# Two transformer blocks on one core: operand casts queued behind the next block's taps, half of a key projection between the scores, first loads on two queues

## The chip, the cores and the metric

One Trainium2 chip (trn2), one of its cores. The metric is the device time of one execution in microseconds, the median of several. Weights and activations are float32.

## What is computed

The reference runs two blocks on one sequence of 256 rows and 1024 columns. The first has two layers of a SwiGLU feed-forward, a mixer of three attentions (stick-breaking, forgetting, memory) with gates and an output projection, and a second SwiGLU feed-forward. The second has a mixer by short causal convolutions, a feed-forward with a three-tap causal convolution (d_ff 2816) before its activation, latent attention (keys and values projected up from a narrow latent, rotary parts apart), and that feed-forward once more.

```python
def _swiglu(t, w_gate, w_up, w_down):
    return (jax.nn.silu(t @ w_gate) * (t @ w_up)) @ w_down
...
        log_beta = jax.nn.log_sigmoid(z)
        log_not = jnp.where(mask, log_beta - z, 0.0)
        log_between = lax.cumsum(log_not, axis=3, reverse=True) - log_not
        w = jnp.where(mask, jnp.exp(log_beta + log_between), 0.0)
```

## The kernel before

All matrix products are taken in float32 accuracy from operands split in two parts, hi + lo, each of type fp32r: product = hi·hi + lo·hi + hi·lo, three matmuls where one would do. A weight travels in chunks of 128x1024: SP issues its DMA into a ring of 5 raw buffers, ACT casts it (`hi`, L270), DVE subtracts (`lo`, L271), into rings of 8. 256 rows make two row blocks t=0, 1. A row-wise product (`mm_a`, L302 to L305, into `acc` banks) takes an operand block as the stationary side and 512 weight columns; a column-wise one (`mm_b`, L313 to L315, into `mm`, `gu` or `cf` banks) gives transposed results of 128 columns by 256 rows. Activations are split likewise: `split` casts on ACT (L392, `acth`) and subtracts (L393, `actl`) on DVE or GpSimd (POOL). Four `mm` banks, two `z` banks for scores and two `tr` banks for transposes make up the eight PSUM banks.

The order on PE is written by a planner, `Program`: steps are generators (`spawn`), which yield a delay in nanoseconds of planned PE time (`DELAY`, L169 to L173), while `tick` advances that time with each matmul issued and `join` makes the main program wait for a step. A larger delay therefore puts more matmuls of the main program in front of a step. The other engines' orders are set by a scheduler, which keeps to a few written rules (`issue_after`).

The places that the change touches:

- The table `DELAY` and `HEAD0` (L169 to L176): `sb_z`, `sb_ln`, `sb_cum`, `sb_last` are the delays of the stick-breaking attention; `lat_p` is one in the latent attention.
- `conv_ffn` (L955 on): 22 blocks c of 2 x 128 columns. `finish` lets ACT do the first tap (`conv3_last`, L893) and DVE the other two (`conv3_rest`, L898), both read from the PSUM bank `cf`, then ACT the activation (L974). `gated` multiplies on GpSimd (L978) and, after a further delay, casts the result for the down-projection (`split`: ACT L392, GpSimd L393). The first four blocks come by another way (a row-wise product and transposes), the other 18 column-wise. The function runs twice, l = 0 and l = 1. After it `out_proj` begins row-wise accumulations in banks that become free.
- `conv_mixer` ends with `out_proj` (L953); `tail` and `head` say how many chunks at the end and the start are done for one row block ahead of the other.
- `latent` (L1078 on): `cols_b(s_uk, ...)` projects eight blocks of keys `kn`, `rows(cq, uqr, 1, 512)` is the rotary query part of t=1. `latent_scores` (L1147, L1150) makes the scores of four units (e, t), head group e and row block t; the softmax is on DVE and ACT (L576), then probabilities are transposed on PE (`tr<-ident,p`, L400), copied by ACT (`pT`, L589), and multiplied with the values (`tr<-pT,mv`, L595).
- `run` (L1196 to L1234) is the start: load the input rows, `ident` (for transposes) and `g`, transpose, and split. `across` (L491) waits for the row scales of a norm.

Of the kernel before, what the change touches and what calls it, by code (L numbers as in the profile page):

```python
# [2 lines left out]

# [1 line left out]

# [4 lines left out]
F32 = mybir.dt.float32  # L10
F32R = mybir.dt.float32r
AF = mybir.ActivationFunctionType
ALU = mybir.AluOpType
# [4 lines left out]
P = 128  # L18
# [3 lines left out]
KD = D // P  # L22
# [107 lines left out]
class Act:  # L130
# [14 lines left out]
    def part(self, k, n, t):  # L145

        ts = slice(t * P, t * P + P)
        return [x[k // 4][:, k % 4:k % 4 + n, ts] for x in (self.hi, self.lo)]
# [10 lines left out]
class Program:  # L159
# [7 lines left out]
    NG = 3  # L167
    FINE = 2
    DELAY = dict(fox_norm=3300, att_norm=3300, lat_norm=3300, f=3000, merge=3000, scale=4500, across=9000, first=4000,  # L169
                 fox_pT=3600, att_pT=3600, lat_pT=3600, sb_z=13000, sb_ln=6000, sb_cum=6000, sb_next=1000, sb_last=13000, sb_w=8000,  # L170
                 decay=8000, fox_gap=7000, fox_p=13900, mem_gap=3000, mem_p=19500, mem_norm=17000, conv0=2200, conv_gap=3000,
                 cf_gap=4100, cf_gated=2000, cf_split=9500, kv=5500, q=4000, rope=5600, lat_gap=6000, lat_p=9000, n_conv=9000,
                 n_ffnA=5500, n_mla=7500, n_ffn10=14900, n_ffn11=8100, n_mix=8300, n_ffn20=8300, n_ffn21=6500)  # L173
    TAIL = 8
    HEAD = 8
    HEAD0 = 1  # L176
    OHEAD = 2
    WARM = 2

# [305 lines left out]
    def across(self, r, ready):  # L485

        rb = self.sp.tile([P, S], F32, tag="rb", bufs=1, name="rb")

        def make():
            nc = self.nc  # L490
            yield from self.wait(*ready, *self.scales)  # L491
            self.scales = []
            ds = []
            for t in range(NT):
                d = self.sp.tile([P, P], F32, tag="diag", bufs=2, name="diag")
                nc.vector.tensor_scalar(out=d, in0=self.ident, scalar1=r[:, t:t + 1], scalar2=None, op0=ALU.mult)
                ds.append(d)
            yield self.DELAY["across"]
            ps = self.tr_bank()
            for t in range(NT):  # L500
                nc.tensor.matmul(ps[:, t * P:t * P + P], self.ones32, ds[t], start=True, stop=True)
            nc.vector.tensor_copy(out=rb, in_=ps[:, :S])

        return rb, self.spawn(make())
# [385 lines left out]
    def conv3_last(self, y, ps, col):  # L890


        self.nc.scalar.mul(out=y, in_=ps, mul=self.pp[:, col + 2:col + 3])  # L893

    def conv3_rest(self, y, ps, col):

# [8 lines left out]
    def conv_mixer(self, x, r, ready, nxt):  # L905
        nc = self.nc
        cols = lambda I, a, b: [I["a_w_in_2"][0][:, D * i + a:D * i + b] for i in (1, 2, 0)]
        head = self.weights("a_in0", KD, 768, lambda I: _side_by_side(cols(I, 0, 256)))
        src = self.weights("a_in", 18, 1024, lambda I: _woven(cols(I, 256, D)))
        dsrc = self.weights("a_out", KD, D, lambda I: _by_k(I["a_w_out_2"][0]))  # L910
        y = Act(self, KD)
        ps = [[self.mm_bank("ca"), self.mm_bank("cb")[:, :S]] for _ in range(NT)]
        outs = [[(p[0], slice(0, 512)), (p[1], slice(512, 768))] for p in ps]
        rows = []

        def first(t):
            cc, p, b = [self.t2(name=n)[:, :S] for n in ("cc", "cp", "cb")]
            nc.scalar.mul(out=cc, in_=ps[t][0][:, :S], mul=r[:, t:t + 1])
            nc.vector.scalar_tensor_tensor(out=p, in0=ps[t][0][:, S:], scalar=r[:, t:t + 1], in1=cc, op0=ALU.mult, op1=ALU.mult)
            nc.scalar.mul(out=b, in_=ps[t][1], mul=r[:, t:t + 1])  # L920
            rows.append((p, b))
            if t:
                self.spawn(second(), self.DELAY["conv0"])

        def finish(c, p, b):
            z = self.t2(name="cz")[:, :S]
            self.conv3(z, p, PP_ACONV + 3 * c)
            nc.vector.tensor_tensor(out=z, in0=b, in1=z, op=ALU.mult)
            return z

        def second():
            for c in range(2):
                s = slice(c * P, c * P + P)
                ps = self.transposed(*[rows[t][i][:, s] for i in range(2) for t in range(NT)]).rearrange("p (i t) q -> p i (t q)", i=2)
                self.split([d[:, 0] for d in y.blocks(c, 1)], finish(c, ps[:, 0], ps[:, 1]), nc.gpsimd)
                yield self.DELAY["conv_gap"]

        rb, made = self.across(r, ready)
        self.rows_a(self.whole(head, KD), outs, x, first, head=self.HEAD, ready=ready)
        self.join(made)  # L940
        for c in range(2, KD):
            bank, bank2 = self.mm_bank("cv"), self.mm_bank("cv")
            parts = [bank[:, :S], bank[:, S:], bank2[:, :S]]
            for i in range(3):
                self.mm_b(parts[i], x, *self.take(src, 3 * (c - 2) + i), KD)
            cc, p = [self.t2(name=n)[:, :S] for n in ("cc", "cp")]
            nc.vector.tensor_tensor(out=cc, in0=parts[0], in1=rb, op=ALU.mult)
            nc.vector.tensor_tensor(out=p, in0=parts[1], in1=cc, op=ALU.mult)
            nc.gpsimd.tensor_tensor(out=p, in0=p, in1=rb, op=ALU.mult)
            z = finish(c, p, parts[2])  # L950
            nc.gpsimd.tensor_tensor(out=z, in0=z, in1=rb, op=ALU.mult)
            self.split([d[:, 0] for d in y.blocks(c, 1)], z, nc.gpsimd)
        return self.out_proj(dsrc, KD, y, None, nxt)  # L953

    def conv_ffn(self, l, x, ready, nxt):  # L955


        nc = self.nc
        cols = lambda I, a, b: [I["ffn_w_up_2"][l][:, DFF * i + a:DFF * i + b] for i in range(2)]
        head = self.weights(f"cf_up0{l}", KD, 1024, lambda I: _side_by_side(cols(I, 0, 512)))  # L960
# [3 lines left out]
        ps, outs = self.banks(2)  # L964
        rows = []

        made = {}

        def finish(c, gu):
            y = self.t2(name="cy", shape=(2, S))  # L970
            for part in (self.conv3_last, self.conv3_rest):
                for i in range(2):
                    part(y[:, i], gu[:, i], PP_FCONV + 132 * l + 3 * (c + KF * i))
            nc.scalar.activation(out=y[:, 0], in_=y[:, 0], func=AF.Silu)  # L974
            made[c] = [self.spawn(gated(c, y), self.DELAY["cf_gated"])]

        def gated(c, y):
            nc.gpsimd.tensor_tensor(out=y[:, 0], in0=y[:, 0], in1=y[:, 1], op=ALU.mult)  # L978
            yield self.DELAY["cf_split"]
            self.split([d[:, 0] for d in hT.blocks(c, 1)], y[:, 0], nc.gpsimd)  # L980

        def first(t):
            gu = [self.t2(name=n) for n in ("cg", "cu")]
# [34 lines left out]
    def latent(self, x, ready, nxt):  # L1018
# [56 lines left out]
        put = lambda dst, eng: (lambda b, ps: eng(out=dst[b // 4][:, b % 4:b % 4 + 2], in_=ps))  # L1075
        self.join(*tkv)
        kn = [self.t4(name="kn") for _ in range(2)]
        self.cols_b(s_uk, range(8), ckv, 2, 4, put(kn, nc.vector.tensor_copy))  # L1078
        self.join(*tq)
        tr.append(self.spawn(qrope(1, rows(cq, uqr, 1, 512))))  # L1080
        qn = [self.t4(name="qn") for _ in range(2)]
# [4 lines left out]
        self.v_done = []  # L1086
        units, second = [[], []], []
        scores = self.spawn(self.latent_scores(units, second, qn, kn, qr, kr, v, x))
        self.cols_b(s_uqn, range(4, 8), cq, 4, 2, put(qn, nc.scalar.copy))
        second.append(True)  # L1090
        ps3, outs3 = self.banks(2)
# [76 lines left out]
    def run(self, out):  # L1168
# [28 lines left out]

        def rows(t):
            for a in range(2):
                cs = slice(a * 512, a * 512 + 512)  # L1200
                nc.sync.dma_start(out=self.h[t][:, cs], in_=xin[t * P:t * P + P, cs])
                if t == a == 0:
                    nc.sync.dma_start(out=self.ident, in_=ident)
                    nc.sync.dma_start(out=g, in_=gd)
            yield 0
            for a in range(2):
                ps = self.transposed(self.h[t][:, a * 512:a * 512 + 512])
                hi, lo = x.part(4 * a, 4, t)
                if t or a:
                    self.split((hi, lo), self.gained(ps, g[:, 4 * a:4 * a + 4]), nc.gpsimd)  # L1210
                    continue
                for i in range(4):
                    gc = g[:, i:i + 1]
                    nc.scalar.mul(out=hi[:, i], in_=ps[:, i], mul=gc)
                    nc.vector.scalar_tensor_tensor(out=lo[:, i], in0=ps[:, i], scalar=gc, in1=hi[:, i].bitcast(F32),
                                                   op0=ALU.mult, op1=ALU.subtract)
            self.scales.append(self.spawn(scale(t), self.DELAY["scale"]))

        def scale(t):
# [4 lines left out]
        def warm(n):  # L1224
            ps = self.z_bank()
            for _ in range(n):
                nc.tensor.matmul(ps[:, :P], self.ones32, self.ones32, start=True, stop=True)

        self.tc.keep_in_program_order(nc.scalar.preload_act_table_set("silu_and_others"))
        ready = [self.spawn(rows(0))]  # L1230
        self.join(*ready)
        warm(self.WARM)
        ready.append(self.spawn(rows(1)))
        self.join(*ready)  # L1234
        state = (x, r, ready)
        for l in range(DEPTH):
            state = self.layer(l, *state, consts if l == 0 else None)
# [102 lines left out]
```

## Time and profile before

| | us |
|---|---|
| median of 3 runs (lowest, highest) | 1896.1 (1895.66, 1896.51) |
| the profiled execution | 1896.99 |
| its span | 1895.2 |
| mean granted TensorE clock, share of full | 0.994 |
| PE, DVE, ACT, POOL busy | 1858.4, 1235.9, 966.7, 228.5 |
| read from HBM | 339.05 MB, 180 GB/s over the span |

Busy times of the four engines are those of the profiled execution. PE's busy time holds all of its matmuls, at whichever clock they ran; the difference to the span, 37 us, is time in which PE stood still. A matmul's duration overlaps that of the next, so work is measured from start to start.

### The profile page before, as it was taken

Reading aid. Unit: us, or ns where it says so; the run is one execution under the profiler, and the core shown is the slowest. Engines: PE = TensorE matmul, PEld = TensorE weight load, DVE = VectorE, ACT = ScalarE, POOL = GpSimd, SP = SyncE. Lnnn points to the kernel's source line nnn. Section 1 sums busy time; section 2 is a strip of 40 time slices with the busy share of each in tenths; the row PEclk is TensorE's granted clock in tenths of the full one; section 3 lists DMA queues with packets and bytes.
Section 4 is the critical chain, followed back from the end, with each engine's and each line's share of the span. In section 5 each row is a group of like instructions: output and inputs, shape, how many; then the busy total and the mean of one; then the engine's idle time right before and its main releaser. Section 6 shows DMA issues by size and latency. Waiting matters only on the chain.

```text
span 1895.2 us, 30338 instructions
## 1 busy us (share of the span) xinstructions
PE 1858.4 (98%) x11982; PEld 1665.5 (88%) x11982; DVE 1235.9 (65%) x1657; ACT 966.7 (51%) x1496; POOL 228.5 (12%) x205
## 2 busy tenths in 40 slices
PE   8999999999999999999999999999999989999988
PEld 7998999778899889989987889988989978779976
DVE  6664756767766476637776776647668656648653
ACT  6444545554644364436555454436456545537552
POOL 1000102001100010001200110001404311003320
PEclk9999999999999999999999999999999999999999
DMA  8655655445555555556533655556555454426551
GB/s 282 220 198 190 222 203 177 143 134 202 210 184 185 178 211 189 181 176 237 186 134 130 214 196 189 185 173 210 183 189 178 167 179 157 148 90 201 172 175 64
DMA packets 95357, 343.13 MB, mean 181 GB/s; under 512 B 10720, under 2 KB 10992, under 8 KB 95216
## 3 DMA queue, kind: packets, MB, share of 16 engines
q1 hardware_dynamic: 95216, 341.20, 52.9%
q8 instruction: 94, 1.54, 0.3%
q14 instruction: 47, 0.39, 0.1%
HBM read 339.05 MB, written 2.11 MB: 180 GB/s over the span
## 4 chain that ended last, share of the span: by engine, by line
PE 39%; DVE 5%; issue 2%; ACT 2%; POOL 2%; DMA 0%; DVEq 0%; POOLq 0%; ACTq 0%
PE acc L302 7%; PE acc L305 7%; PE acc L303 6%; DVE cy L898 2%; POOL cy L978 2%; PE gu L314 2%; PE gu L315 2%; PE gu L313 2%; DVE lo L271 2%; ACT hi L270 2%; PE cf L314 2%; PE cf L315 2%; PE cf L313 2%; PE tr L400 1%; PE cv L314 1%
## 5 line engine op out<-in xcount | busy, mean ns | idle before, releaser
L271 DVE TENSOR_TENSOR lo<-raw,hi 128x1024 fp32r<-128x1024 f32 (+3 forms) x609 | 748.0, 1236 | 360.9 <-ACT hi L270 359.6
L270 ACT CAST hi<-raw 128x1024 fp32r<-128x1024 f32 (+3 forms) x609 | 633.1, 1044 | 439.6 <-PE acc L305 212.4
L302 PE MATMUL acc<-hi,acth 128*128 128x512 f32 x1176 | 473.8, 403 | 13.5 <-DVE cy L898 11.8
L303 PE MATMUL acc<-lo,acth 128*128 128x512 f32 x1176 | 466.3, 396 | 0.2 <-DVE lo L271 0.2
L305 PE MATMUL acc<-hi,actl 128*128 128x512 f32 x1176 | 378.9, 397 | 1.8 <-DVE actl L393 1.8
L315 PE MATMUL gu<-acth,lo 128*128 128x256 f32 x1152 | 324.0, 281 | 0.0
L314 PE MATMUL gu<-actl,hi 128*128 128x256 f32 x1152 | 323.8, 281 | 0.0
L313 PE MATMUL gu<-acth,hi 128*128 128x256 f32 x1152 | 323.5, 281 | 0.0
L302 PEld LDWEIGHTS acc<-hi,acth 128*128 128x128 f32 x1176 | 222.8, 189 | 68.0 <-ACT cy L974 13.5
L305 PEld LDWEIGHTS acc<-hi,actl 128*128 128x128 f32 x1176 | 221.9, 189 | 55.8 <-DVE actl L393 4.1
L303 PEld LDWEIGHTS acc<-lo,acth 128*128 128x128 f32 x1176 | 222.9, 190 | 49.5 <-DVE lo L271 0.9
L313 PEld LDWEIGHTS gu<-acth,hi 128*128 128x128 f32 x1152 | 217.1, 188 | 0.2
L314 PEld LDWEIGHTS gu<-actl,hi 128*128 128x128 f32 x1152 | 217.0, 188 | 0.2
L315 PEld LDWEIGHTS gu<-acth,lo 128*128 128x128 f32 x1152 | 217.0, 188 | 0.0
L417 POOL TENSOR_TENSOR r<-v,mhalf 128x1 f32<-128x1 f32 x40 | 52.9, 1322 | 966.9 <-DVE v L414 955.9
L313 PE MATMUL cf<-acth,hi 128*128 128x256 f32 x576 | 162.3, 282 | 0.0
L315 PE MATMUL cf<-acth,lo 128*128 128x256 f32 x576 | 162.1, 281 | 0.0
L314 PE MATMUL cf<-actl,hi 128*128 128x256 f32 x576 | 161.9, 281 | 0.0
L313 PE MATMUL mm<-acth,hi 128*128 128x256 f32 x432 | 122.7, 284 | 0.0
L314 PE MATMUL mm<-actl,hi 128*128 128x256 f32 x432 | 121.6, 281 | 0.0
L315 PE MATMUL mm<-acth,lo 128*128 128x256 f32 x432 | 121.5, 281 | 0.0
L313 PEld LDWEIGHTS cf<-acth,hi 128*128 128x128 f32 x576 | 108.7, 189 | 0.1
(225 smaller groups left out, 2285.6 us busy)
## 6 DMA issues: line engine op xcount, KB each, us to landing
raw<-ffn_gu SPq DMA_DIRECT2D x175, 512.0 KB, 4.3
raw<-ffn_dn SPq DMA_DIRECT2D x88, 512.0 KB, 3.3
raw<-cf_up SPq DMA_DIRECT2D x88, 512.0 KB, 3.5
raw<-gate SPq DMA_DIRECT2D x48, 512.0 KB, 3.3
raw<-cf_dn SPq DMA_DIRECT2D x44, 512.0 KB, 3.5
raw<-a_in SPq DMA_DIRECT2D x18, 512.0 KB, 4.7
gain<-gains SPq DMA_DIRECT2D x17, 512.0 KB, 4.7
raw<-in_v SPq DMA_DIRECT2D x16, 516.0 KB, 4.4
```

The source lines that it names most:

```text
L270: self.last_hi = nc.scalar.copy(out=hi[:, cs], in_=raw[:, cs])
L271: nc.vector.tensor_tensor(out=lo[:, cs], in0=raw[:, cs], in1=hi[:, cs].bitcast(F32), op=ALU.subtract)
L302: nc.tensor.matmul(ps, x.h(k, ts), hi[:, cs], start=first, stop=False)
L303: nc.tensor.matmul(ps, x.h(k, ts), lo[:, cs], start=False, stop=False)
L305: nc.tensor.matmul(ps, x.l(k, ts), hi[:, cs], start=False, stop=last)
L313: nc.tensor.matmul(ps, hi[:, c], x.h(k), start=k == 0, stop=False)
L314: nc.tensor.matmul(ps, hi[:, c], x.l(k), start=False, stop=False)
L315: nc.tensor.matmul(ps, lo[:, c], x.h(k), start=False, stop=k == nk - 1)
L400: self.nc.tensor.transpose(ps[:, w * P:w * P + P], n[:, c * P:c * P + P], self.ident)
L417: nc.gpsimd.tensor_tensor(out=r, in0=v, in1=self.mhalf, op=ALU.pow)
L898: self.nc.vector.scalar_tensor_tensor(out=y[:, i:], in0=ps[:, :S - i], scalar=self.pp[:, col + 2 - i:col + 3 - i], in1=y[:, i:], op0=ALU.m ...
L978: nc.gpsimd.tensor_tensor(out=y[:, 0], in0=y[:, 0], in1=y[:, 1], op=ALU.mult)
```

## The change

Six edits. In `conv_ffn` the cast of block c's product (`split` in `gated`) is issued behind the taps of block c+1 on ACT, if those are known. In `latent`, key blocks 4 to 7 are projected after the scores have been spawned, and `lat_p` is a microsecond of planned time shorter. Four stick-breaking delays are longer. `conv_mixer`'s output projection has tail 6 and head 2. `across` waits first for the operands and then for the scales. At the start, `ident`, `g` and the second row block are loaded by ACT's queue, all four quarters are split by the plain `split` (low halves on DVE), the second row block's transposes are a step with a delay of its own that isn't joined, and `HEAD0` is 3.

```diff
-                 fox_pT=3600, att_pT=3600, lat_pT=3600, sb_z=13000, sb_ln=6000, sb_cum=6000, sb_next=1000, sb_last=13000, sb_w=8000,
+                 fox_pT=3600, att_pT=3600, lat_pT=3600, sb_z=13500, sb_ln=7000, sb_cum=7000, sb_next=1000, sb_last=15000, sb_w=8000,
...
-                 cf_gap=4100, cf_gated=2000, cf_split=9500, kv=5500, q=4000, rope=5600, lat_gap=6000, lat_p=9000, n_conv=9000,
-                 n_ffnA=5500, n_mla=7500, n_ffn10=14900, n_ffn11=8100, n_mix=8300, n_ffn20=8300, n_ffn21=6500)
+                 cf_gap=4100, cf_gated=2000, cf_split=9500, kv=5500, q=4000, rope=5600, lat_gap=6000, lat_p=8000, n_conv=9000,
+                 start=1300, n_ffnA=5500, n_mla=7500, n_ffn10=14900, n_ffn11=8100, n_mix=8300, n_ffn20=8300, n_ffn21=6500)
...
-    HEAD0 = 1
+    HEAD0 = 3
...
-            yield from self.wait(*ready, *self.scales)
+            yield from self.wait(*ready)
+            yield from self.wait(*self.scales)
...
-        self.nc.scalar.mul(out=y, in_=ps, mul=self.pp[:, col + 2:col + 3])
+        self.last_tap = self.nc.scalar.mul(out=y, in_=ps, mul=self.pp[:, col + 2:col + 3])
...
-        return self.out_proj(dsrc, KD, y, None, nxt)
+        return self.out_proj(dsrc, KD, y, None, nxt, tail=6, head=2)
...
-        made = {}
+        made, taps = {}, {}
...
+            taps[c] = self.last_tap
             nc.scalar.activation(out=y[:, 0], in_=y[:, 0], func=AF.Silu)
             made[c] = [self.spawn(gated(c, y), self.DELAY["cf_gated"])]
...
             yield self.DELAY["cf_split"]
-            self.split([d[:, 0] for d in hT.blocks(c, 1)], y[:, 0], nc.gpsimd)
+            with self.tc.issue_after(taps[c + 1].ins) if c + 1 in taps else nullcontext():
+                self.split([d[:, 0] for d in hT.blocks(c, 1)], y[:, 0], nc.gpsimd)
...
-        self.cols_b(s_uk, range(8), ckv, 2, 4, put(kn, nc.vector.tensor_copy))
+        self.cols_b(s_uk, range(4), ckv, 2, 4, put(kn, nc.vector.tensor_copy))
...
         scores = self.spawn(self.latent_scores(units, second, qn, kn, qr, kr, v, x))
+        self.cols_b(s_uk, range(4, 8), ckv, 2, 4, put(kn, nc.vector.tensor_copy))
...
             for a in range(2):
-                cs = slice(a * 512, a * 512 + 512)
-                nc.sync.dma_start(out=self.h[t][:, cs], in_=xin[t * P:t * P + P, cs])
-                if t == a == 0:
-                    nc.sync.dma_start(out=self.ident, in_=ident)
-                    nc.sync.dma_start(out=g, in_=gd)
+                ps = self.transposed(self.h[t][:, a * 512:a * 512 + 512])
+                self.split(x.part(4 * a, 4, t), self.gained(ps, g[:, 4 * a:4 * a + 4]))
             yield 0
-            for a in range(2):
-                ps = self.transposed(self.h[t][:, a * 512:a * 512 + 512])
-                hi, lo = x.part(4 * a, 4, t)
-                if t or a:
-                    self.split((hi, lo), self.gained(ps, g[:, 4 * a:4 * a + 4]), nc.gpsimd)
-                    continue
-                for i in range(4):
-                    gc = g[:, i:i + 1]
-                    nc.scalar.mul(out=hi[:, i], in_=ps[:, i], mul=gc)
-                    nc.vector.scalar_tensor_tensor(out=lo[:, i], in0=ps[:, i], scalar=gc, in1=hi[:, i].bitcast(F32),
-                                                   op0=ALU.mult, op1=ALU.subtract)
...
+        nc.scalar.dma_start(out=self.ident, in_=ident)
+        nc.scalar.dma_start(out=g, in_=gd)
+        for t, a in ((0, 0), (0, 1), (1, 0), (1, 1)):
+            cs = slice(a * 512, a * 512 + 512)
+            (nc.scalar if t else nc.sync).dma_start(out=self.h[t][:, cs], in_=xin[t * P:t * P + P, cs])
...
         warm(self.WARM)
-        ready.append(self.spawn(rows(1)))
-        self.join(*ready)
+        ready.append(self.spawn(rows(1), self.DELAY["start"]))
```

What moves on ACT in the middle of the convolutional feed-forward, between one block's taps (`cy<-cf,pp`) and the next's. Before (line numbers after the change are one to four higher):

```order
L893 ACTIVATE cy<-cf,pp 128x256 x2
L270 CAST hi<-raw 128x1024
L974 ACTIVATE cy<-cy 128x256
L392 CAST acth<-cy 128x256
L270 CAST hi<-raw 128x1024
L893 ACTIVATE cy<-cf,pp 128x256 x2
```

With the change:

```order
L894 ACTIVATE cy<-cf,pp 128x256 x2
L392 CAST acth<-cy 128x256
L270 CAST hi<-raw 128x1024
L976 ACTIVATE cy<-cy 128x256
L270 CAST hi<-raw 128x1024
L894 ACTIVATE cy<-cf,pp 128x256 x2
```

The operand cast has moved from behind its block's activation to behind the next block's taps; the two weight casts are still there, one on either side of the activation.

The second place is ACT at the end of the latent scores: `p` is a softmax activation, `z_16603` and `z_16604` (before) and `z_16599` and `z_16600` (after) are the scores of the last unit, `pT` the copies of transposed probabilities, `acth` the operand of the output projection. Before:

```order
L576 ACTIVATE p_16572,sums_16571<-z_16552,m_16570 128x128 x2
L589 COPY pT_16615<-tr_16616 128x256
L589 COPY pT_16620<-tr_16621 128x256
L589 COPY pT_16625<-tr_16626 128x512
L589 COPY pT_16632<-tr_16633 128x512
L576 ACTIVATE p_16641,sums_16640<-z_16603,m_16639 128x256 x2
L392 CAST acth_16397<-tr_16659 128x2x128
L576 ACTIVATE p_16648,sums_16647<-z_16604,m_16646 128x256 x2
L392 CAST acth_16397<-tr_16664 128x2x128
```

With the change:

```order
L1099 COPY mv_16358<-acc11_16516 128x512
L270 CAST hi_16827<-raw_16826 128x1024
L577 ACTIVATE p_16613,sums_16612<-z_16599,m_16611 128x256 x2
L577 ACTIVATE p_16620,sums_16619<-z_16600,m_16618 128x256 x2
L590 COPY pT_16625<-tr_16626 128x256
L590 COPY pT_16630<-tr_16631 128x256
L590 COPY pT_16635<-tr_16636 128x512
L590 COPY pT_16642<-tr_16643 128x512
L392 CAST acth_16359<-tr_16655 128x2x128
```

The last unit's softmax activations have moved ahead of the four copies; the casts of the first results follow without an activation between them.

The third place is PE at the same scores. `z` are the scores of the second head group, first of t=0 (128x128), then of t=1 (128x256), and `acc` the value projection between them. Before:

```order
L1150 MATMUL z<-kr,qr 128x128 x2
L302 MATMUL acc_16519<-hi,acth 128x512
L303 MATMUL acc_16519<-lo,acth 128x512
L302 MATMUL acc_16520<-hi,acth 128x512
L303 MATMUL acc_16520<-lo,acth 128x512
L305 MATMUL acc_16519<-hi,actl 128x512
L305 MATMUL acc_16520<-hi,actl 128x512
L1147 MATMUL z<-kn,qn 128x256 x2
```

With the change the first six accumulations read the same, and twelve more follow before the scores, of which the last six and the scores are:

```order
L302 MATMUL acc_16515<-hi,acth 128x512
L303 MATMUL acc_16515<-lo,acth 128x512
L302 MATMUL acc_16516<-hi,acth 128x512
L303 MATMUL acc_16516<-lo,acth 128x512
L305 MATMUL acc_16515<-hi,actl 128x512
L305 MATMUL acc_16516<-hi,actl 128x512
L1151 MATMUL z<-kn,qn 128x256 x2
```

Eighteen accumulations now lie between the two pairs of scores, where there were six.

## Rows read from the trace of the kernel before

**Rows 1.** The page, part 1: busy us, share of the span, instructions.

```profile
PE 1858.4 (98%) x11982; PEld 1665.5 (88%) x11982; DVE 1235.9 (65%) x1657; ACT 966.7 (51%) x1496; POOL 228.5 (12%) x205
```

**Rows 2.** PE's waits over the whole run: us in total, times, longest us.

```profile
PE acc L302 <- DVE cy L898: 11.8, 3, 5.5
...
PE tr L641 <- DVE lnl L393: 1.7, 4, 0.6
PE acc L302 <- ACT acth L392: 1.6, 3, 0.7
...
PE z L609 <- DVE lnl L393: 0.9, 2, 0.4
```

**Rows 3.** Timeline of PE, conv_ffn's end: start, us, operation, xcount, [idle before <-releaser].

```profile
1523.11 0.63 PE L305 MATMUL acc<-hi,actl 128*128 128x512 f32 x2
...
1524.17 0.39 PE L303 MATMUL acc<-lo,acth 128*128 128x512 f32 x1
1530.02 0.77 PE L302 MATMUL acc<-hi,acth 128*128 128x512 f32 x1 [5.47 <-DVE cy L898]
```

**Rows 4.** Timeline of ACT, the last block of the same loop.

```profile
1520.54 0.83 ACT L893 ACTIVATE cy<-cf,pp 128x256 f32<-128x256 f32 x2
...
1525.45 0.40 ACT L392 CAST acth<-cy 128x256 fp32r<-128x256 f32 x1 [2.14 <-POOL cy L978]
1525.76 1.04 ACT L270 CAST hi<-raw 128x1024 fp32r<-128x1024 f32 x1
1526.71 0.83 ACT L893 ACTIVATE cy<-cf,pp 128x256 f32<-128x256 f32 x2
1529.07 0.42 ACT L974 ACTIVATE cy<-cy 128x256 f32<-128x256 f32 x1 [1.52 <-DVE cy L898]
```

**Rows 5.** Timeline of DVE, the last block's two other taps.

```profile
1527.98 1.90 DVE L898 SCALAR_TENSOR_TENSOR cy<-cf,pp,cy 128x255 f32<-128x255 f32 x4
```

**Rows 6.** Table of stretches: us, PE, PEld, DVE, ACT, POOL (instructions), PEclk, DMA share, GB/s.

```profile
1500.00:1518.00 18.00, 18.00 (x154) 18.00 (x154) 11.74 (x19) 10.34 (x18) 6.41 (x7) 1.00 0.50 171
...
1530.00:1534.20 4.20, 4.18 (x10) 3.33 (x11) 1.02 (x1) 1.45 (x2) 1.45 (x2) 0.50 0.15 60
...
1650.30:1653.50 3.20, 3.20 (x10) 1.72 (x10) 0.74 (x2) 0.00 (x0) 0.00 (x0) 0.50 0.48 164
...
1831.40:1834.50 3.10, 3.09 (x7) 2.46 (x8) 0.00 (x0) 1.41 (x2) 1.47 (x2) 0.50 0.22 89
1691.00:1694.60 3.60, 3.60 (x10) 2.79 (x11) 3.06 (x4) 0.00 (x0) 1.46 (x1) 0.53 0.86 279
```

**Rows 7.** Timeline of PE, the stick-breaking sums of the first layer.

```profile
342.90 0.51 PE L641 MATMUL tr<-lnh,tri 128*128 128x512 f32 x1 [0.34 <-ACT lnh L392]
343.94 0.51 PE L641 MATMUL tr<-lnl,tri 128*128 128x512 f32 x1 [0.54 <-DVE lnl L393]
```

**Rows 8.** Timeline of PE, the last latent scores.

```profile
1647.45 0.70 PE L1147 MATMUL z<-kn,qn 128*128 128x256 f32 x2 [0.70 <-ACT p L576]
1649.59 0.70 PE L1147 MATMUL z<-kn,qn 128*128 128x256 f32 x2 [1.43 <-ACT p L576]
```

**Rows 9.** Timeline of ACT, first copies of probabilities and the last softmax activations.

```profile
1654.64 0.65 ACT L589 COPY pT<-tr 128x256 f32<-128x256 f32 x2 [5.11 <-PE tr L400]
...
1656.78 0.49 ACT L576 ACTIVATE p<-z,m 128x256 f32<-128x256 f32 x1
```

**Rows 10.** Timelines of PE and DVE, transposes of the query's second row block.

```profile
1613.00 0.60 PE L400 MATMUL tr<-ident,nrm 128*128 128x128 f32 x4
...
1615.44 0.68 DVE L393 TENSOR_TENSOR actl<-tr,acth 128x512 fp32r<-128x512 f32 x1
```

**Rows 11.** Timeline of PE, the start of the second convolutional feed-forward.

```profile
1690.85 0.95 PE L305 MATMUL acc<-hi,actl 128*128 128x512 f32 x2 [0.88 <-DVE actl L393]
```

**Rows 12.** Timelines of SP (DMA issues) and PE at the start.

```profile
2.10 1.38 SPq L1201 DMA_DIRECT2D h<-x  x3
...
11.01 0.78 PE L302 MATMUL acc<-hi,acth 128*128 128x512 f32 x1
```

More of the change, by code (lines that the diff above doesn't have):

```diff
@@ L1 @@
 import math
-from contextlib import ExitStack
+from contextlib import ExitStack, nullcontext
 import numpy as np
```

## The prediction

> **What bounds the kernel now.** I read the engines' busy times first: TensorE (PE) is busy 98% of the span, the next engine 65% [rows 1]. The change takes no matmul away, so it can win only the time in which PE stands still and what it loses at half clock. The list of PE's waits comes second: 11.8 us in three waits at one line, then waits of 1 to 3 us in all at each of several places [rows 2]. Third come the timelines around these waits and the table of stretches. Its column PEclk is the granted clock: 1.00, the 2.4 GHz level, in a stretch without gaps, and 0.50 to 0.53, the 1.2 GHz level, for 4.2, 3.1, 3.2 and 3.6 us behind places where PE had just stood idle [rows 6]. Half of such a stretch is lost, so each wait is priced together with the slow stretch behind it.
>
> The sum is made against the profiled execution, 1896.99 us; the median of the three runs is 0.9 us lower, so I take the saving off 1896.1. A measurement of this kernel can tell about 0.2% (3.8 us) from no change.
>
> **1. The casts in the convolutional feed-forward (15.4 us).** It runs twice. For blocks 4 to 21, 18 in each, PE does 48 matmuls of 128x256, 5.6 us (18 us for 154 of them, 0.117 each [rows 6]). ACT starts to empty a block's bank with its taps (L893), and DVE's two other taps free it [rows 5]. ACT's cycle is longer than PE's: taps start at 1520.54 and at 1526.71, 6.17 us apart, though the work in between is 0.83 + 0.42 + 0.40 and two weight casts of 1.04, 3.7 us. The rest is ACT standing still, 2.14 us of it in the operand cast, which waits for GpSimd's product with a weight cast and the next taps queued behind it [rows 4]. A lag of 0.57 us per block gives 10 us in 18 blocks, and so late the last bank comes free. PE has 24 accumulations to do in the other banks, 5.6 us (two take 0.63 with 0.39 for one, so 0.235 each), ends them at 1524.5 and stands 5.47 us, until 1530.02 [rows 3]; the second pass shows the same wait with one of 0.86 ahead of it, 11.8 in all [rows 2].
>
> The change holds the cast of block c back until the taps of block c+1. The product was there 4.9 us after its block's taps (1525.45 - 1520.54); the next taps come 5.6 us after them, and the cast 6.4 us, so it meets a finished product with 1.5 us to spare, and ACT's cycle falls towards its 3.7 us of work, below PE's 5.6: ACT follows PE. From the start of the last taps to PE's restart the trace has 3.3 us (1526.71 to 1530.02); with a weight cast of 1.04 in front the bank is free 4.3 us after the last block, inside the 5.6 us of accumulations. So 11.8 us of waits go, and half of the slow stretches of 4.2 and 3.1 us: 3.65. **Gain 15.4.** Ends: 8 if half the lag stays, 15.8 with the ragged restart. The cover: the cast, and two weight casts a block behind it, now wait in ACT for PE's next block. By the order of instructions eight weight chunks are cast ahead of each taps, as before, and a block uses two, so PE doesn't feel it. GpSimd's subtraction for the low half moves a block later too; its reader comes tens of us later, and the last block, which has no next taps, isn't held.
>
> **2. Stick-breaking delays (4.5 us).** PE waits 1.7 + 0.9 us for DVE's log terms [rows 2] and 0.34 in each of two layers for ACT's [rows 7], 3.3 in all. A wait costs about half as much again at the restart: from 342.90 to 343.94 are 1.04 us where 0.235 is usual, 0.8 lost for a wait of 0.54. That makes 4.8. By the order the new delays put six or more matmuls, 0.7 to 1.4 us, before each place, more than any one wait. What follows in the mixer comes some 7 us later, and 12 us of accumulations still stand before its last gate, 19 before. **Gain 4.5**, ends 2 and 4.8.
>
> **3. The start (1.3 us).** Each DMA issue costs SP 0.46 us (three in 1.38). `ident`, `g` and the second row block leave its queue, so the second half of the first block is issued 0.9 us sooner and the weights 1.8 us sooner; the first accumulation, now at 11.01 us, no longer has the second block's transposes ahead of it [rows 12]. The bytes are the same. **Gain 1.3**, ends -0.5 (ACT issues four DMAs ahead of its table load) and 3. The Trainium skill, "DMA: Bandwidth & Descriptors", section "Issuing engines are not separate DMA queues", says that transfers started by several engines share the same 16 DMA engines and interleave, and that only the time of issuing is saved. If by that sentence the first loads are limited by transfer, this part is worth 0 and the sum is 1872.8; no row here shows two issuing engines.
>
> **4. From the convolution mixer to its feed-forward (1.0 us).** PE's waits for ACT's operand casts are 1.6 us in three [rows 2], one of them here, 0.7, with two smaller ones behind it. Head 2 and tail 6 leave 36 instead of 48 accumulations behind the first row block and bring the second's transposes 15 rows forward. Ends -1 (less cover for the first norm) and 1.9 (all); I take the middle on the side of a gain, since the casts stand behind weight casts that come sooner now.
>
> **5. From the latent attention to its feed-forward (2.4 us).** Another 0.7 of those casts, then 0.88 us for the low halves [rows 11], then 3.6 us at 0.53, of which 1.7 are lost [rows 6]. Twelve more accumulations (2.8 us) of the second row block now stand behind the first one's end, to cover its norm. All of it would be 3.2; I take 2.4, ends 0 and 3.2.
>
> **6. The latent scores (0).** Saved: PE waits 0.70 and 1.43 us before the last scores [rows 8], as the softmax of the scores before still holds the banks. Half of the key projection moves behind the scores' start, so 18 accumulations (4.2 us) stand there instead of 6 (1.4). The 3.2 us at 0.50 behind it give 1.6 [rows 6]. Together 3.7. Added: ACT runs the last scores' four softmax activations, about 0.6 us each from 1656.78, ahead of the probabilities' copies, which stood at 1654.64 [rows 9]. PE's products need these copies, so they come 3.0 us later; as the activations no longer lie among the later copies and casts, 1.3 come back: +1.7. Transposes and products alternate in other pieces: +0.5. And the key projection's 24 matmuls (2.8 us) are gone from in front of the query's second row block: only 9 follow its transposes, so PE wants the operand at 1613.60 + 9 x 0.117 = 1614.7, and DVE ended it at 1616.12 [rows 10]; with one copy less on DVE I take +1.1 of the 1.4. The clock may fall behind such a wait: half of the 1.6, +0.8. So 4.1 against 3.7: I take **0**; ends a loss of 5 (nothing saved but the waits, all added prices and a slow stretch as before) and a gain of 4.
>
> **Sum:** 15.4 + 4.5 + 1.3 + 1.0 + 2.4 + 0 = 24.6; 1896.1 - 24.6 = **1871.5 us**. The parts lie in different stages, so they add.
>
> **Rivals.**
> *Latent attention gets worse.* The copies behind the activations cost the end of part 6. For: the order puts four activations first; against: PE has 2.8 us more of other work near there. 1871.5 + 5 = 1876.5.
> *The feed-forward's waits only halve.* ACT also waits 1.52 us in its block for DVE's taps [rows 4], and this stays. Against: without the 2.14 its cycle is 6.17 - 2.14 = 4.0, below 5.6. Gain 8 instead of 15.4: 1879, up to 1883 with the clock.
> *Two queues give nothing,* by part 3: 1872.8. For: the same bytes; against: 1.8 us of issuing are gone from SP.
> *All is cured,* upper ends of parts 1 to 5 and half of part 6's: 15.8 + 4.8 + 3 + 1.9 + 3.2 + 2 = 30.7, 1865.5.
> *Slower: weight casts stuck behind a cast that waits for PE.* Place: ACT in the 36 blocks. If fewer than two weight chunks were cast ahead at the taps, PE would stand each block for taps, cast and weight cast, 0.83 + 0.40 + 1.04 = 2.27 us [rows 4], 82 us in all: 1953. That number of two decides. Against: the order has eight, in both programs.
>
> **How the numbers follow.** Forecast 0.50 (1867 to 1875.5); two queues give nothing 0.12; latent worse 0.17; halved 0.11; all cured 0.07; slower 0.03. The range leaves out the slower case, the far half of the halved one and some of the tails: 1863.5 to 1881. Faster by over 0.2% is everything but the slower case and a tail of the halved one in which the small parts turn: 0.95; within 0.2%: 0.02; slower 0.03.
>
> **What would show it.** Right: accumulations wait under 1 us in all on `cy`, ACT's taps stand 5.6 us apart, and no 0.50 stretch follows either pass; PE's waits on the log terms are below 1 us; the first accumulation starts near 9.5 us; the waits before the last latent scores are gone, and one of 2 to 3 us on the copies of the probabilities has come. Wrong: taps still 6 us apart, weight casts that PE waits for in the blocks, or over 5 us lost between the latent scores and the output projection.

## The result and the profile after

| | before | changed |
|---|---|---|
| median (lowest, highest), us | 1895.92 (1895.66, 1896.51) | 1877.58 (1876.01, 1878.95) |
| profiled execution, us | 1896.99 | 1876.01 |

The ratio is 0.9903, 95% interval 0.9885 to 0.9920: 18.3 us faster, 15.2 to 21.8 by the interval. 24.6 us were forecast. The changed kernel's four runs lie 3 us apart and the profiled one is the fastest, so the profile's own saving, 21.0 us, is on the high side. One execution of c_only below took 2258.49 us at a granted clock of 0.753; its figures are those of the other three.

The engines of the changed kernel, page, part 1 [rows 1]:

```profile
PE 1850.2 (99%) x11982; PEld 1664.7 (89%) x11982; DVE 1241.3 (66%) x1658; ACT 965.8 (52%) x1493; POOL 228.5 (12%) x202
```

PE's waits of the changed kernel (us in all, times, longest) [rows 2]:

```profile
PE tr L400 <- DMA ident<-ident: 4.4, 1, 4.4
PE acc L302 <- ACT acth L392: 4.3, 3, 1.7
PE tr L400 <- ACT pT L590: 3.5, 1, 3.5
PE lat L305 <- DVE actl L393: 1.1, 1, 1.1
PE acc L302 <- DVE cz L929: 1.0, 1, 1.0
```

The 11.8 us on `cy` and all waits on the log terms (`lnl`, `lnh`) are gone. New are 3.5 us on the copies of probabilities, 1.1 us in the latent projection, 1.0 us on `cz` in the convolution mixer, and 2.7 us more for ACT's operand casts.

PE where the feed-forward's blocks end in the down-projection; before, 5.47 us of waiting and 4.2 us at half clock lay here [rows 3]:

```profile
1514.73 0.40 PE L302 MATMUL acc<-hi,acth 128*128 128x512 f32 x1
...
1519.84 0.63 PE L305 MATMUL acc<-hi,actl 128*128 128x512 f32 x2
```

ACT near the end of the same loop [rows 4]:

```profile
1502.99 0.83 ACT L894 ACTIVATE cy<-cf,pp 128x256 f32<-128x256 f32 x2
1503.71 0.40 ACT L392 CAST acth<-cy 128x256 fp32r<-128x256 f32 x1
1504.86 1.05 ACT L270 CAST hi<-raw 128x1024 fp32r<-128x1024 f32 x1 [0.75 <-PE cf L314]
1505.82 0.41 ACT L976 ACTIVATE cy<-cy 128x256 f32<-128x256 f32 x1
1507.74 1.05 ACT L270 CAST hi<-raw 128x1024 fp32r<-128x1024 f32 x1 [1.51 <-PE cf L314]
1508.69 0.83 ACT L894 ACTIVATE cy<-cf,pp 128x256 f32<-128x256 f32 x2
```

Taps stand 5.70 us apart instead of 6.17, the cast waits for nothing, and ACT now stands idle until PE's matmuls release a weight buffer (`<-PE cf`): it is ahead of PE, not late.

The table of stretches of the changed kernel (PE, PEld, DVE, ACT, POOL, PEclk, DMA, GB/s) shows the clock behind both passes and at the start of the second feed-forward at 1.00 where rows 6 had 0.50 to 0.53. Behind the new latent wait it is 0.69:

```profile
1518.00:1530.00 12.00, 12.00 (x53) 9.72 (x52) 6.13 (x5) 5.66 (x6) 1.18 (x2) 1.00 0.47 162
1815.00:1825.00 10.00, 10.00 (x44) 8.07 (x44) 6.13 (x5) 4.34 (x5) 0.00 (x0) 1.00 0.77 254
1643.00:1646.00 3.00, 2.64 (x16) 2.11 (x13) 1.02 (x2) 1.52 (x4) 0.00 (x0) 0.69 0.00 0
1678.00:1682.00 4.00, 3.88 (x17) 3.19 (x18) 3.05 (x6) 2.11 (x5) 1.63 (x1) 1.00 0.91 364
```

### The profile page after: what moved, and what is told of

Its sections match the earlier page's. It is cut to its first block, busy times and chain, and to the rows that moved or that the text cites. A ratio compares the mean times of both kernels' runs of the same rounds, so it can differ in the third digit from the quotient of the medians.

```text
span 1873.9 us, 30344 instructions
## 1 busy us (share of the span) xinstructions
PE 1850.2 (99%) x11982; PEld 1664.7 (89%) x11982; DVE 1241.3 (66%) x1658; ACT 965.8 (52%) x1493; POOL 228.5 (12%) x202
## 4 chain that ended last, share of the span: by engine, by line
PE 94%; DVE 3%; issue 2%; ACT 1%; DMA 1%; POOL 0%; DVEq 0%; POOLq 0%; ACTq 0%
PE acc L302 14%; PE acc L305 14%; PE acc L303 14%; PE gu L314 7%; PE gu L315 7%; PE gu L313 7%; PE cf L314 4%; PE cf L315 4%; PE cf L313 4%; PE mm L313 3%; PE mm L315 3%; PE mm L314 3%; PE tr L400 2%; DVE lo L271 1%; PE tr L596 1%
## 5 line engine op out<-in xcount | busy, mean ns | idle before, releaser
L302 PE MATMUL acc<-hi,acth 128*128 128x512 f32 x1176 | 472.5, 402 | 5.3 <-ACT acth L392 4.3
L302 PEld LDWEIGHTS acc<-hi,acth 128*128 128x128 f32 x1176 | 221.3, 188 | 58.8 <-ACT acth L392 6.0
```

The costliest lines, as they stand in the source:

```text
L302: nc.tensor.matmul(ps, x.h(k, ts), hi[:, cs], start=first, stop=False)
```

## The experiments

Twelve kernels in three groups of four, each group on one chip with the kernel before beside it (medians 1896.74, 1896.57, 1896.55). "Saved" is against that median. An edit undone in the changed kernel is compared with the changed kernel's second measurement, `again`.

Differences of 2 to 3 us between these kernels need care, because the start of the program varies by as much from profile to profile. In the first feed-forward 825 matmuls into `gu` follow each other without a matmul of another kind. I divide every profile at the first of them. The first of these lines is from the changed kernel's first profile, the second from again, the third from no_head, and up to there all three run the same instructions:

```profile
40.29 0.37 PE L313 MATMUL gu<-acth,hi 128*128 128x256 f32 x1
...
42.38 0.36 PE L313 MATMUL gu<-acth,hi 128*128 128x256 f32 x1
...
39.94 0.37 PE L313 MATMUL gu<-acth,hi 128*128 128x256 f32 x1
```

Profiles by this division (the runs are explained below):

| profile | first of these matmuls at, us | from there to the start of the last matmul, us |
|---|---|---|
| before | 41.5 | 1846.5 |
| changed, first profile | 40.3 | 1826.4 |
| changed, again | 42.4 | 1826.0 |
| c_only | 42.4 | 1829.4 |
| no_c | 39.7 | 1843.5 |
| sb_only | 41.6 | 1838.3 |
| no_sb | 40.4 | 1833.7 |
| no_lat | 41.5 | 1826.0 |
| late400 | 40.8 | 1822.4 |
| no_head | 39.9 | 1825.6 |
| no_start | 41.8 | 1823.7 |
| one_queue | 42.4 | 1827.0 |
| act_ident | 42.6 | 1847.3 |
| best | 42.5 | 1821.9 |

Each row is the one profiled execution; of the others only the whole time is known. The changed kernel's two rows agree to 0.4 us in the last column and differ by 2.1 in the one before it.

**The casts alone (c_only).** The kernel before with this edit:

```diff
-            self.split([d[:, 0] for d in hT.blocks(c, 1)], y[:, 0], nc.gpsimd)
+            with self.tc.issue_after(taps[c + 1].ins) if c + 1 in taps else nullcontext():
+                self.split([d[:, 0] for d in hT.blocks(c, 1)], y[:, 0], nc.gpsimd)
```

> The kernel before with one edit: the feed-forward's operand cast held behind the next block's taps. Theory (ACT's cycle in the blocks is the whole cause): the waits on cy and the half-clock stretches behind both passes go, 15.9 us by the loss of the rows of before, so ratio 0.9916, about 1880. Rival (the other edits share in it, or the wait moves elsewhere on ACT): a gain of 8 us or less, ratio 0.996.

Median 1878.94 us, ratio 0.9909 (0.9894 to 0.9925): 17.8 us saved, nearly as much as by all six edits, and 17.0 in the last column of the table. No wait on `cy` is left in PE's list. The theory holds. One thing it did not name: at the start of the second feed-forward c_only keeps the two waits of before, 0.66 and 0.89 us, but PE is not at half clock behind them, where before the second of these lines took 0.63 us:

```profile
1684.49 0.73 PE L305 MATMUL acc<-hi,actl 128*128 128x512 f32 x2 [0.89 <-DVE actl L393]
1685.06 0.39 PE L302 MATMUL acc<-hi,acth 128*128 128x512 f32 x1
```

**All but the casts (no_c).** The changed kernel with a plain `split`.

> The changed kernel without the held cast. Theory: the other edits together are worth what is left of the measured 18.3 us, 2.5 to 7 us: ratio 0.997 to 0.9987, and the waits of 5.5 us on cy are back in both passes. Rival (the parts overlap): ratio below 0.995.

1892.77 us, ratio 0.9983 (0.9974 to 0.9992): the five other edits save 4.0 us where 9.2 were forecast, as the theory said. PE's waits are back as they were:

```profile
PE acc L302 <- DVE cy L899: 11.6, 3, 5.5
```

So the shortfall lies in the small parts, and the next runs take them up.

**The stick-breaking delays alone, and undone (sb_only, no_sb).**

```diff
-sb_z=13000, sb_ln=6000, sb_cum=6000, sb_next=1000, sb_last=13000
+sb_z=13500, sb_ln=7000, sb_cum=7000, sb_next=1000, sb_last=15000
```

> The kernel before with the four new stick-breaking delays alone. Theory (they take the 2.4 us of loss out of each layer): 4 to 5.5 us faster than before, ratio 0.997 to 0.998, with no wait on log terms over 0.3 us. Rival (half comes back later in the mixer): 2 us, ratio 0.999.

> The changed kernel with the four stick-breaking delays as before. Theory (the delays remove the waits on the log terms and nothing takes their place): the 2.4 us of loss in each layer are back, 4 to 5 us slower than the changed kernel. Rival (part of it is given back by what comes later in the mixer): 1 to 2.5 us slower.

Alone 1889.79 us, ratio 0.9962 (0.9950 to 0.9975), 6.8 us saved; undone 1883.13 us, 5.6 us above the changed kernel of the same group. By the table sb_only saves 8.1 us behind the start and no_sb loses 7.3 to 7.7; the smaller 5.6 comes from comparing with again, whose profile starts 2.0 us later than that of no_sb. With the delays no wait on a log term is in PE's list. By the starts of same-numbered matmuls sb_only gains 3.6 us on the kernel before in each layer's mixer, 2.7 to 2.8 of them around the sums and the rest in what follows, where nothing was forecast. The term of 4.5 was too small, and the rival (half comes back later) is out.

**The latent edits undone (no_lat).**

```diff
-        self.cols_b(s_uk, range(4), ckv, 2, 4, put(kn, nc.vector.tensor_copy))
+        self.cols_b(s_uk, range(8), ckv, 2, 4, put(kn, nc.vector.tensor_copy))
...
-        self.cols_b(s_uk, range(4, 8), ckv, 2, 4, put(kn, nc.vector.tensor_copy))
```

(and `lat_p` 9000.)

> The changed kernel with the latent attention's two edits undone (all eight key blocks before the scores, lat_p 9000). Theory (latent edits exchange two waits of 2.1 us and a slow stretch for one wait of 3.5 us on the copies and one of 1.1 us): within 1.5 us of the changed kernel, 1876 to 1879. Rival (they are a loss that eats the rest of the forecast): 3 to 5 us faster, 1873 to 1875. Rival (they are a gain): slower by 3 us.

1876.42 us, ratio 0.9894 (0.9881 to 0.9908), beside 0.9903 of the changed kernel: no difference that the runs can tell, and none behind the start by the table (1826.0 against 1826.0 and 1826.4). The two waits went and others came, as reckoned, though not in the sizes reckoned. PE and ACT of the changed kernel [rows 8, 9]:

```profile
1638.43 0.66 PE L400 MATMUL tr<-ident,p 128*128 128x128 f32 x4
1642.57 1.09 PE L400 MATMUL tr<-ident,p 128*128 128x128 f32 x8 [3.48 <-ACT pT L590]
```

```profile
1640.32 0.47 ACT L577 ACTIVATE p<-z,m 128x256 f32<-128x256 f32 x1 [3.44 <-DVE m L575]
...
1641.68 0.48 ACT L577 ACTIVATE p<-z,m 128x256 f32<-128x256 f32 x1
...
1642.13 0.66 ACT L590 COPY pT<-tr 128x256 f32<-128x256 f32 x2
```

PE's transposes were done at 1639.1. ACT stood idle for 3.44 us; first in its queue were the activations of the last scores, which waited for DVE's maximum until 1640.32 and then took 1.8 us. The copies that PE wanted were behind them.

**The last softmax 400 ns later (late400).** The changed kernel and:

```diff
+        if e and t:
+            yield self.DELAY["lat_late"]
         p, sums = self.softmax(z, 2, n, 192.0 ** -0.5)
```

> The changed kernel with one step more: the softmax of the last latent scores (second head group, second row block) starts after 400 ns more of planned PE time, so that ACT copies the first four transposed probabilities ahead of those softmax activations, as before the change. Theory (the 3.5 us wait of PE's transposes on the copies comes from the activations in front of them, about 2.2 us of work and the wait for DVE's maximum): that wait falls under 0.7 us and the time by 2.5 to 3.5 us, to 1874 to 1875. Rival (the copies wait for something else, or the last softmax becomes late by as much): no change, 1877.

1873.67 us, ratio 0.9881 (0.9867 to 0.9894), 2.75 us under no_lat in the same group and 3.9 under the changed kernel's first median; behind the start it is 3.6 to 4.0 us shorter than the changed kernel. The theory holds. The wait has shrunk from 3.48 to 0.30 us, and nothing came in its place but the 0.93 that was there before the change. PE of late400:

```profile
1639.71 1.09 PE L400 MATMUL tr<-ident,p 128*128 128x128 f32 x8 [0.30 <-ACT pT L590]
...
1643.22 2.34 PE L596 MATMUL tr<-pT,mv 128*128 128x128 f32 x16 [0.93 <-DVE actl L393]
```

So the place of four activations in ACT's order made 3.2 of the 3.48 us of this wait.

**The changed kernel again (again).**

> The changed kernel once more, on the chip of the three others of this job, with a profile of its own. Theory (the gain is 18 to 21 us, and the runs of one kernel differ by 2 to 3 us through how long PE stays at half clock behind its waits): median 1876 to 1879, losses at the same places as in the first profile. Rival (the first four runs were a poor sample of a gain of 24): 1872 to 1873.

1877.56 us, ratio 0.9903 (0.9889 to 0.9916), so the gain is 18 to 19 us. The theory holds. The places of loss are the same, but the wait on `cz` is 0.35 us instead of 0.95, and the start differs. Elsewhere in the run an accumulation takes 0.39 to 0.40 us where the granted clock is 1.00 and 0.63 or more where it is 0.50. At the start I go by these durations, because the table's clock is 1.00 there in some profiles although accumulations take 0.63. In the first profile the short ones begin at 12.7 us; in this one some come early, and they are back for good only at 17.4. The table and the timeline of again:

```profile
13.00:17.00 4.00, 4.00 (x15) 3.31 (x15) 1.63 (x3) 2.00 (x5) 0.00 (x0) 0.50 0.89 325
```

```profile
13.11 0.63 PE L302 MATMUL acc<-hi,acth 128*128 128x512 f32 x1
...
14.82 1.91 PE L400 MATMUL tr<-ident,h 128*128 128x128 f32 x8
...
17.38 0.47 PE L302 MATMUL acc<-hi,acth 128*128 128x512 f32 x1
```

After the change, in the first profile:

```profile
8.97 0.79 PE L302 MATMUL acc<-hi,acth 128*128 128x512 f32 x1 [1.74 <-ACT acth L392]
...
13.08 0.39 PE L302 MATMUL acc<-hi,acth 128*128 128x512 f32 x1
...
14.01 1.04 PE L400 MATMUL tr<-ident,h 128*128 128x128 f32 x8
```

In again the accumulations at 8.09 and 8.43 us took 0.50 and 0.40; then PE waited 0.63 and 0.23 us for weight operands, and the granted clock fell. That these waits made it fall is not shown: no_c, with the same start, waited 0.27, 0.22 and 0.76 us there, and its accumulations kept to 0.40 and 0.50. By the first of the 825 matmuls the two profiles are 2.1 us apart; the changed kernel's eight executions lie between 1876.01 and 1878.95 us.

**The convolution mixer's projection undone (no_head).**

```diff
-        return self.out_proj(dsrc, KD, y, None, nxt, tail=6, head=2)
+        return self.out_proj(dsrc, KD, y, None, nxt)
```

> The changed kernel with the convolution mixer's output projection as before (tail 8, head 0). Theory (the edit costs: a new wait of 1.0 us for cz near 1363 us, and the wait for the cast near 1384 us grew to 1.3): the first wait goes, the second returns to 0.7 to 0.9, 0.5 to 1.5 us faster than the changed kernel. Rival (the prediction's term): 1 us slower.

1874.75 us, 2.8 us under again: the edit costs, but less than that. PE of the changed kernel shows the price, first profile and then the first of the two places in again:

```profile
1364.41 0.50 PE L302 MATMUL acc<-hi,acth 128*128 128x512 f32 x1 [0.95 <-DVE cz L929]
...
1385.73 0.50 PE L302 MATMUL acc<-hi,acth 128*128 128x512 f32 x1 [1.13 <-ACT acth L392]
```

```profile
1365.96 0.50 PE L302 MATMUL acc<-hi,acth 128*128 128x512 f32 x1 [0.35 <-DVE cz L929]
```

PE without the edit, no_head, at the second place:

```profile
1383.41 0.50 PE L302 MATMUL acc<-hi,acth 128*128 128x512 f32 x1 [0.30 <-ACT acth L392]
...
1384.79 0.73 PE L305 MATMUL acc<-hi,actl 128*128 128x512 f32 x2 [0.18 <-DVE actl L393]
```

no_head has no wait at the first place. The waits are 1.6 us longer with the edit in the first profile (0.95 + 1.13 against 0.30 + 0.18) and 1.0 in again, whose second wait is 1.13 too. Over the whole run behind the start the edit is worth 0.4 us (again) to 0.8 (first profile) in the table. The two profiled executions, both within 0.2 us of their medians, are 2.9 us apart, and 2.4 of these stand already at the start, 42.4 against 39.9 us, where both run the same instructions.

**The start undone (no_start).** The changed kernel with the old `rows`, loads on SP alone, `HEAD0` 1 and the joint wait in `across`.

> The changed kernel with the start as before (all loads on SP, the second row block's transposes before the first accumulations, HEAD0 1, operands and scales waited for together). Theory (first accumulation 2.0 us later, of which the transposes moved behind it take back 0.9): 1.0 to 1.3 us slower. Rival (the loads are limited by transfer): no difference.

1874.32 us, 3.2 us under again: neither theory nor rival, the new start costs. At the first of the 825 matmuls no_start is 1.5 us behind the first profile of the changed kernel, which is the theory's 1.0 to 1.3 and a little more, and 0.6 ahead of again. The loss comes after the start: from there on no_start is 2.3 to 2.7 us shorter. Those 825 matmuls of 128x256 fill one window without waits (PE, PEclk, DMA, GB/s): the kernel before, then no_start, then the changed kernel:

```profile
43.00:138.00 95.00, 95.00 (x806) 1.00 0.63 207
```

```profile
43.00:138.00 95.00, 95.00 (x806) 1.00 0.63 208
```

```profile
43.00:138.00 95.00, 95.00 (x804) 1.00 0.60 207
```

Two matmuls less in 95 us at the same granted clock. From the start of the first to that of the last, the 825 take 97.43 us in before and no_start and 97.79 in the changed kernel. 800 matmuls from about 610 us take 135.14 and 135.38 us. Summed over all pairs of neighbouring matmuls behind the 400th that start within 0.26 us of each other in both traces, the changed kernel takes 2.5 us more than no_start: it is some 0.2% slower without a wait, and this is about as much as was lost behind the start.

**One queue, and a second queue in the kernel before (one_queue, act_ident).** The changed kernel with the start's loads on `nc.sync`; and the kernel before with

```diff
-                    nc.sync.dma_start(out=self.ident, in_=ident)
+                    nc.scalar.dma_start(out=self.ident, in_=ident)
```

> The changed kernel with its first loads back on SP's queue alone (first half of the first block, ident, g, the other three halves, then weights); the rest of the new start stays. In the profiles so far every kernel with loads on ACT's queue needs 135.38 us for the same 800 matmuls in the stretch from about 610 us, every kernel without 135.14: 0.18% in a stretch without waits, some 2.7 us over the run. Theory (a second queue in use makes PE's matmuls start that much further apart for the whole run): 135.14 us here, and 1874 to 1876, 1.5 to 3 us faster than the changed kernel although the start itself comes 1 us later. Rival (another part of the new start does it, the splits or the delayed second row block): 135.38 and 1877 to 1879.

> The kernel before with one word changed: ident is loaded by ACT's queue, everything else as it was. Theory (a second queue in use slows the matmuls of the whole run): the stretch of 800 matmuls takes 135.38 instead of 135.14 us, and the kernel is 1.5 to 3 us slower than before, ratio 1.0008 to 1.0016. Rival: the stretch keeps 135.14 us, and the kernel is within 1 us of before.

The theory fell. one_queue has 135.38 us in the stretch, as the changed kernel, and takes 1879.16 us, 1.6 more than again. Its first accumulation starts at 10.46 us, that of again at 8.09, but again loses this at half clock, and both reach the 825 matmuls at 42.4: the 1.6 us are not the start's. In the traces 1.0 us lie behind it, 0.6 at the wait on `cz` and most of the rest in a longer half-clock stretch behind the latent scores, neither of which the edit touches. act_ident has 135.21, between the two, and 1897.70 us, ratio 1.0001 (0.9992 to 1.0010). Which part of the edits that no_start undoes together sets the pace (the splits, the transposes behind the first accumulations, `HEAD0`, the two waits in `across`) and by what means stays open.

**Three steps put right (best).** The changed kernel with one_queue's loads, no_head's projection and late400's softmax.

> The changed kernel with three steps put right: first loads on SP's queue alone, the convolution mixer's output projection as before (tail 8, head 0), and the last latent softmax 400 ns later. Theory (the parts add: 2 for the queue, 1.1 to 2.8 for the projection, 3 to 4 for the softmax): 1868.5 to 1871.5. Rival (they overlap): 1872 to 1874.

1873.04 us, ratio 0.9872 (0.9858 to 0.9885), 23.5 us saved, 4.5 more than the changed kernel again. It beats both kernels, by the rival's figure and not the theory's. Putting the loads back on one queue gained nothing: the slower pace stays, and the profile reaches the 825 matmuls at 42.5 us. From there on best has the shortest time of all, but its median can't be told from that of late400 alone (0.9858 to 0.9885 and 0.9867 to 0.9894). Late softmax, old projection and old start together, which these runs suggest, was not run.

## Why the prediction was right, and where its terms were off

The sign and the range held (1863.5 to 1881); the median is 6.1 us above the forecast. The largest term was right in cause and nearly in size. That the small terms did no more harm is in part luck: two terms too low made up for about half of four that were too high. Where a place is priced below, I compared the starts of same-numbered matmuls in the first traces of the two kernels, ahead of the place and behind it.

1. *Casts, 15.4.* Right in cause and size: 16.2 at the two places, 17.8 measured alone, and in the trace 11.8 us of waits and the two slow stretches are gone. ACT's cycle follows PE, the cover of eight chunks held, and the slower rival did not come: in the blocks ACT waits for PE to free weight buffers.
2. *Stick-breaking, 4.5.* Right in cause, too low: 7.1 in the two mixers of sb_only, beyond the upper end of 4.8. The working put what follows the sums at nothing; it gave 0.8 to 0.9 in each layer, and why stays open.
3. *Start, +1.3.* The step failed. "The first accumulation no longer has the second block's transposes ahead of it" came true: 8.97 us instead of 11.01, and the first profile is 1.2 us ahead of the kernel before at the 825 matmuls. But the term ended there. It lacked two things: a pace of matmuls 0.2% slower for the whole run, 2.5 us, and a start whose slow accumulations end anywhere from 12.7 to 17.4 us, so that again is 0.9 us behind the kernel before at the 825 matmuls. Together that is a loss of 1.3 in the first profile, and no_start's median is 3.2 under that of again. The end of -0.5 was too near; no row of before could have shown it. The Trainium skill's sentence from "DMA: Bandwidth & Descriptors", section "Issuing engines are not separate DMA queues", allows the time of issuing alone. The traces agree with it on average: the seven profiles with two queues reach the 825 matmuls at 39.7 to 42.4 us, 40.7 in the mean, and the two of the new start with one queue at 42.4 and 42.5, 1.8 us later, as much as the issuing that SP was spared. With a spread of 2.7 us among the seven this is no proof.
4. *Convolution mixer, +1.0.* Wrong sign: a loss of 0.9 us at the place in the first profile, of 0.4 to 0.8 against no_head behind the start. "The middle on the side of a gain" was a lean without a row; with head 2 PE waits for a bank that DVE still reads for `cz`, which the working did not look for.
5. *Second feed-forward, 2.4.* 1.9 us were gained here, but the named cause holds for little of it. The second wait went and the first grew from 0.66 to 1.46 us. The slow stretch went too (1.5 to 1.7 us), but it is also gone in c_only, sb_only and no_lat, which keep both waits. So the edits gave some 0.4 us, and the term counted as theirs a slow stretch that can come or stay away behind the same waits.
6. *Latent scores, 0.* Right within its ends, and by the mechanism named: no_lat can't be told from the changed kernel. Against the kernel before the place lost 1.3 us. The wait for the copies was 3.5 us; 2 to 3 were said, and the activations' own wait for DVE's maximum, 1.2 us behind the transposes' end, was not in the sum.

With sb_only's figure for the delays this is, place by place, 16.2 + 7.1 - 1.3 - 0.9 + 1.9 - 1.3 = 21.7 us; the last matmul starts 21.3 us earlier in the changed kernel's trace. The forecast was 24.6: terms 1 and 2 were 3.4 too low, terms 3 to 6 together 6.3 too high. The medians show 18.3 and not 21 because the profiled execution of the changed kernel is 1.6 us under its median and that of the kernel before 1.1 above.

## What to carry to other kernels

ACT's queue, which casts for two consumers in order, ran late by a wait (2.14 us in a cycle of 6.17) and not by its work (3.7): put the cast whose input comes late behind the next item that is ready anyway, and check how many items stand between. After each move of work ask what now stands first in the other engine's queue: four activations waiting for a maximum held up copies that were ready. A term for which no row speaks should carry its whole spread, to either side. Where the start varies by 2 us from profile to profile, compare kernels from a matmul behind it, and not by medians alone.

## What was not expected of the hardware

In stretches without a wait, at a granted clock of 1.00, the same matmuls run at three paces, which go with the way the program begins: 135.14 us for 800 of them in the kernel before, c_only, sb_only and no_start, 135.21 in act_ident, and 135.38 in all that have the new start with its edit in `across`, in all three groups of runs. It is in single instructions: from the first of three accumulations (L302) to its neighbour are 232.8 ns on average in the changed kernel and 231.4 in no_start, and in the two others the means differ by 0.3 or less. The second DMA queue was ruled out as the cause, since one_queue keeps the slow pace; the cause stays open.
